# SSD's weighted inputs as broadcast products on GpSimd, and four loads of the merge on ScalarE's queue

## The chip, the cores and the metric

The kernel runs on one core of a Trainium2 chip. Its time is device microseconds of one execution; of several runs the median is given. The engines are TensorE (PE), VectorE (DVE), ScalarE (ACT), GpSimd (POOL) and SyncE (SP). Each takes its instructions in order from a queue of its own, and waits for the others by semaphores. SyncE only issues DMAs here; ScalarE and GpSimd issue some among their own work.

## The reference, cut to what matters

One step of a hybrid layer on 576 frames (512 of a prompt and 64 of a sample), width 1024, float32:

```python
h = x + 0.5 * swiglu(rmsnorm(x, norm_ffn1), w_ffn1_in, w_ffn1_out)
h = h + mixer(rmsnorm(h, norm_mix))
h = h + 0.5 * swiglu(rmsnorm(h, norm_ffn2), w_ffn2_in, w_ffn2_out)
# mixer(u):
parts = split_cols(u @ w_in, IN_SIZES)          # one projection for three branches and three gates
merged = (sigmoid(g_ssd) * (y_ssd @ w_proj_ssd) + sigmoid(g_att) * (y_att @ w_proj_attn)
          + sigmoid(g_ml) * (y_ml @ w_proj_mlstm))
return merged @ w_out
# one chunk of the SSD scan (16 heads of 64 in 4 groups, state 128), per group and head:
y = (cb * lmat * dtc) @ xc + exp(cum) * (cc @ h)
wd = exp(last - cum) * dtc
h = exp(last) * h + einsum('bsh,bsn,bshp->bhpn', wd, bc, xc)
```

The change concerns the last two lines, where each input row is weighted by `wd` before it is multiplied into the state, and the start of the sum `merged`.

## The kernel before

The program runs through a first feed-forward (to some 600 us), the mixer's input projection with the three branches (to 1210), the merge with its output projection, and a second feed-forward. Frames lie along the free axis as 512 + 64 columns, or in two halves of 288.

Every large product is made of three: the weight and the activation are each split into a rounded part and a rest (`split`, L288 a cast on ScalarE and L289 a subtraction on VectorE; `ph`, `pl` for weights, `TH`, `TL` for activations), and `acc` collects TH x ph, TL x ph and TH x pl in L616. The projection saves multiplications by working on two tiles at a time with seven sums of weight blocks (as Strassen does). The sums come from an accumulating DMA (L461) and from additions on GpSimd (L472, `wy`); SyncE loads the raw blocks (L467, L237 into `wr`) some operands ahead, into rings of 5 (`wr`), 4 (`wx`), 2 (`wy`) and 6 (`ph`, `pl`). When a product's bank is complete, it is emptied by ScalarE (`uv`, L533, or `g`, L540) or by VectorE (L542); TensorE takes the bank again a few products later.

The branches are generators. While the projection for later tiles runs, a job of attention (a), mLSTM (m) or SSD (s) advances by one `yield` after each product (`tick`, L575), in the order a0 a1 m0 s0 a2 a3 s1 m1 s2 m2 s3 m3. This is the order in which the code is written; a scheduler then reorders each engine's instructions by modelled times, so that an edit in one place can change the order of all engines.

`ssd(g)` does one group of the SSD in two halves j of two heads (8 halves in all). Line numbers are those of the kernel before: the weights `wd` come from rows that a DMA brings from DRAM (`R<-scr_rows`, L181, L1175) by L1209 and L1210 on VectorE and an Exp on ScalarE; x is transposed (L1218, L1222) and multiplied by dt into `xd` (L1219, L1223); L1228 makes the weighted copy `xw` on ScalarE; L1234 to L1237 and L1242 make decay factors on ScalarE, L1238 and L1239 multiply them on GpSimd. The state matmul L1252 reads `xw`, L1255 and L1260 update the state, L1274 to L1287 make the output. Other work that stands near: L1049 masks of mLSTM (VectorE, from `R`), L1152 the convolution's last step (ScalarE).

`merge()` multiplies the branches' outputs, stored in DRAM as `ys`, by the three projections. Its first four loads (`heads(0, 1, 2, 3)`, L1340) bring attention's outputs, 288 KB each; they are split into YH and YL (L288, L289) for the products L260. GpSimd loads the gates beside it (`g<-gs`, L1354).

Of the kernel before, what the change touches and what calls it, by code (L numbers as in the profile page):

```python
# [27 lines left out]
AF = mybir.ActivationFunctionType  # L28
ALU = mybir.AluOpType
# [5 lines left out]
CH = [(0, 128), (128, 128), (256, 128), (384, 128), (512, 64)]  # L35
# [46 lines left out]
class Hybrid:  # L82
# [1085 lines left out]
    def ssd(self, g, t):  # L1168
        nc = self.nc
# [12 lines left out]
        h4 = lambda ap: ap.rearrange("p c (h e) -> p c h e", e=64)  # L1182
# [4 lines left out]
        for c in range(4):  # L1187
# [3 lines left out]
                                op=ALU.mult)  # L1191
# [7 lines left out]
        for j in range(2):  # L1199
# [4 lines left out]
            wd = self.unit([128, 5, 2], "wd", 2)  # L1204
            el = self.unit([128, 5, 2], "el", 2)
            nc.gpsimd.memset(wd[:, 4, :], 0.0)
            for r in range(2):
# [3 lines left out]
                                        op=ALU.subtract)  # L1211
# [3 lines left out]
            xd, xw = self.t("t", (128, 5, 128)), self.t("t", (128, 5, 128))  # L1215
            ps = self.ps("x")
            for c in range(4):
# [4 lines left out]
            nc.tensor.transpose(ps[:64, :128], x[:, 515:579], self.ident)  # L1222
            nc.vector.tensor_tensor(h4(xd[:64, 4:5, :]), ps[:64, :128].rearrange("p (c h e) -> p c h e", h=2, e=64),  # L1223
                                    self.TM[:64, 4:5, d0:d0 + 2].unsqueeze(3).broadcast_to([64, 1, 2, 64]), op=ALU.mult)
            for c, (a, n) in enumerate(CH):
                for r in range(2):
                    hs = slice(r * 64, (r + 1) * 64)
                    nc.scalar.activation(xw[:n, c, hs], xd[:n, c, hs], AF.Copy, scale=wd[:n, c, r:r + 1])  # L1228

            for r in range(2):  # L1230
                e = cum[r]
# [14 lines left out]
            for c, (a, n) in enumerate(CH):  # L1246
# [9 lines left out]
                else:  # L1256
                    h = states[c]
                    for r in range(2):
                        hs = slice(r * 64, (r + 1) * 64)
# [68 lines left out]
    def merge(self):  # L1328
        nc, tc = self.nc, self.tc
        def rows():  # L1330
            return [Rows(self.mp.tile([128, T], F32R, name=f"Y{v}", tag=f"{v}{i}", bufs=1) for i in range(8)) for v in "HL"]

        ys = [self.mp.tile([128, T], F32, name="y", tag="y", bufs=4) for _ in range(4)]
        YH, YL = rows()
        merged = self.mp.tile([128, 8, T], F32, name="merged")
        ZH, ZL = [Rows(self.xp.tile([128, T], F32R, name=f"Z{v}{i}") for i in range(8)) for v in "HL"]

        def load(src, eng=nc.gpsimd):
            y = ys.pop() if ys else self.mp.tile([128, T], F32, name="y", tag="y", bufs=4)
            eng.dma_start(y, src)  # L1340
            return y


        gates = deque((8 * b + n) for b in (1, 2, 0) for n in range(8))
        loaded = deque()

        def fill(n):
            while gates and len(loaded) < n:
                i = gates.popleft()
                if i in STAY:  # L1350
                    y = self.stay[i]
                else:
                    y = self.t("g")
                    self.last = nc.gpsimd.dma_start(y, self.gs[i]).ins  # L1354
                loaded.append((i, y))

        def put(n, branch):

            box = {}

            def go(h, ps, sl):
                if not box:
                    i, box["t"] = loaded.popleft()
                    assert i == 8 * branch + n
                    fill(5)
                t = box["t"][:, sl]
                o = merged[:, n, sl] if branch == 1 else t
                nc.vector.scalar_tensor_tensor(o, t, 1.0, ps, op0=ALU.add, op1=ALU.mult)
                if branch != 1:
                    nc.gpsimd.tensor_tensor(merged[:, n, sl], merged[:, n, sl], t, op=ALU.add)  # L1370
            return go

        def heads(*which, eng=nc.gpsimd):
            for i in which:
                y = load(self.ys[i], eng)
                if i < 4:
                    self.split(y, YH[:, i, :], YL[:, i, :])
                else:
                    self.scaled(y, C_ML - 4, YH, YL, i, slice(0, T), tile=True)

        def half(branch, which):
            w = ("w_proj_attn", "w_proj_mlstm")[branch - 1]
            for m in which:
                self.gemm([((w, 0, 512, m * 256, 256), [(e * 128, put(2 * m + e, branch)) for e in range(2)])],
                          YH, YL, k0=4 * branch - 4)

        def ssd(which):

            for k in which:
                y = load(self.ys[8 + k])  # L1390
                nc.vector.scalar_tensor_tensor(y, y, self.cst[:, C_GS + k:C_GS + k + 1], self.rs,
                                               op0=ALU.mult, op1=ALU.mult)
                self.split(y, ZH[:, k, :], ZL[:, k, :])

        with tc.high_priority(offset=1500):
            heads(0, 1, 2, 3, eng=nc.sync)
        fill(5)
        half(1, (0, 1))
        heads(4, 5, 6)
        half(1, (2, 3))  # L1400
        heads(7)
        ssd(range(2))
        half(2, (0, 1))
        ssd(range(2, 5))
        half(2, (2, 3))
        ssd(range(5, 8))
        tiles = [(("w_proj_ssd", 0, 1024, n * 128, 128), [(0, put(n, 0))]) for n in range(8)]
        self.gemm(tiles[:4], ZH, ZL)

        with tc.issue_after(self.last):  # L1410
            for k in range(0, 8, 2):
                nc.gpsimd.dma_start(self.R1[:, k:k + 2, :], self.xs[:, k:k + 2, :])
        self.gemm(tiles[4:5], ZH, ZL)
        self.gemm(tiles[5:], ZH, ZL, half_major=True)
        XH, XL = rows()
        for a, n in HALVES:
            for k in range(8):
                sl = slice(a, a + n)
                self.split(merged[:, k, sl], XH[:, k, sl], XL[:, k, sl])

        def res(n):
            def go(h, ps, sl):

                nc.vector.scalar_tensor_tensor(self.R1[:, n, sl], ps, 0.5, self.R1[:, n, sl], op0=ALU.mult, op1=ALU.add)
            return go
        tiles = [(("w_out", 0, 1024, n * 128, 128), [(0, res(n))]) for n in range(8)]
        self.gemm(tiles[:3], XH, XL, half_major=True)
        self.gemm(tiles[3:5], XH, XL)
        self.gemm(tiles[5:], XH, XL, half_major=True)
# [179 lines left out]
```

## Time and profile before

| what | value |
|---|---|
| median of 3 runs | 1942.54 us (1939.22 to 1944.31) |
| profiled execution: time, span | 1944.79 us, 1943.1 us |
| TensorE busy, mean granted clock | 1887.2 us (97%), 0.991 |
| VectorE, ScalarE, GpSimd busy | 1524.6 us (78%), 1089.5 us (56%), 680.1 us (35%) |
| mean DMA rate | 152 GB/s |

The profile is of one execution. A row of a timeline gives the start, the time that the group of like instructions took, what it was, how often, and in brackets how long the engine stood idle just before and what released it. A row `PE acc <- ACT uv` among the waits says that TensorE stood until ScalarE's `uv` copy had emptied a bank. The granted clock is a share of full speed. What stands idle or slow on TensorE adds to the time nearly one for one here, since it is busy for 97% of the span.

### The profile page before, as it was taken

The page shows a single profiled execution, that of the slowest core. Times are in us where ns is not written, and L with a number is a line of the kernel's source. Part 1 is how long each engine was busy: PE and PEld are TensorE (multiplying, and loading weights), DVE is VectorE, ACT ScalarE, POOL GpSimd, SP SyncE. Part 2 cuts the span into 40 slices and gives each one's busy share as a digit, 9 for nine tenths or more (in the row PEclk, how much of TensorE's full clock was granted, in tenths as well). Part 3 has the DMA queues.
Part 4 walks back from the last instruction along what each step waited for, and adds up shares of the span by engine and source line. Part 5 has one row for each costly group of instructions (what it writes and reads, how often), then busy time and mean ns, then how long its engine had stood idle before and what let it go on. Part 6 is the DMA issues. An engine that isn't in the chain of part 4 may idle for free. (4 is left out here: it accounts for less than half of the span.)

```text
span 1943.1 us, 37678 instructions
## 1 busy us (share of the span) xinstructions
PE 1887.2 (97%) x13901; PEld 1823.6 (94%) x13901; DVE 1524.6 (78%) x2715; ACT 1089.5 (56%) x2486; POOL 680.1 (35%) x656
## 2 busy tenths in 40 slices
PE   9999999999999999999999998999999999999998
PEld 8899999999999878888888888999999999999998
DVE  8998998988768767667777775745898888988865
ACT  4554654655544777767675765324555455554544
POOL 5343333333202234323435353440233334334311
PEclk9999999999999999899999999999999999999999
DMA  7267666666742545753667557742236666666631
GB/s 241 74 160 173 159 163 163 159 172 163 185 131 80 156 117 159 200 147 108 183 165 183 155 152 213 241 143 88 77 99 165 163 157 172 166 157 167 159 94 60
DMA packets 129440, 294.69 MB, mean 152 GB/s; under 512 B 14289, under 2 KB 26193, under 8 KB 129257
## 3 DMA queue, kind: packets, MB, share of 16 engines
q1 hardware_dynamic: 100072, 205.67, 32.7%
q0 software_dynamic: 19696, 72.10, 20.5%
q10 hardware_dynamic: 9488, 14.53, 2.6%
q8 instruction: 109, 1.79, 0.4%
q14 instruction: 75, 0.61, 0.1%
HBM read 272.87 MB, written 19.38 MB: 150 GB/s over the span
## 5 line engine op out<-in xcount | busy, mean ns | idle before, releaser
L616 PE MATMUL acc<-TH,ph 128*128 128x288 f32 x3220 | 968.0, 301 | 27.4 <-ACT uv L533 11.8
L616 PE MATMUL acc<-TL,ph 128*128 128x288 f32 x3220 | 955.4, 297 | 0.6 <-DVE TL L289 0.6
L616 PE MATMUL acc<-TH,pl 128*128 128x288 f32 x3220 | 955.0, 298 | 1.0 <-DVE pl L289 0.9
L616 PEld LDWEIGHTS acc<-TH,ph 128*128 128x128 f32 x3220 | 607.5, 189 | 46.9 <-ACT uv L533 15.5
L616 PEld LDWEIGHTS acc<-TL,ph 128*128 128x128 f32 x3220 | 609.4, 189 | 4.9 <-issue 3.7
L616 PEld LDWEIGHTS acc<-TH,pl 128*128 128x128 f32 x3220 | 608.4, 189 | 4.8 <-DVE pl L289 2.2
L289 DVE TENSOR_TENSOR pl<-wr,ph 128x512 fp32r<-128x512 f32 x471 | 429.4, 919 | 76.9 <-ACT ph L288 64.5
L288 ACT CAST ph<-wr 128x512 fp32r<-128x512 f32 x471 | 287.9, 620 | 267.9 <-PE acc L616 141.3
L289 DVE TENSOR_TENSOR pl<-wx,ph 128x512 fp32r<-128x512 f32 x390 | 328.1, 845 | 44.5 <-ACT ph L288 37.9
L288 ACT CAST ph<-wx 128x512 fp32r<-128x512 f32 x390 | 237.4, 621 | 201.3 <-POOL wx L472 110.2
L472 POOL TENSOR_TENSOR wx<-wx,wr 128x512 f32<-128x512 f32 x160 | 246.3, 1539 | 188.2 <-DVE pl L289 150.4
L461 POOL DMA_DIRECT2D wx<-in_sblk x115 | 101.6, 901 | 524.1 <-DMA wx<-in_sblk 154.7
L260 PE MATMUL acc<-YH,ph 128*128 128x256 f32 (+1 forms) x768 | 226.5, 298 | 6.3 <-ACT YH L288 5.8
L260 PE MATMUL acc<-YL,ph 128*128 128x320 f32 (+1 forms) x768 | 227.1, 297 | 2.3 <-DVE YL L339 1.9
L260 PE MATMUL acc<-YH,pl 128*128 128x256 f32 (+1 forms) x768 | 226.5, 296 | 0.1
L260 PEld LDWEIGHTS acc<-YH,ph 128*128 128x128 f32 x768 | 145.4, 190 | 6.9 <-ACT YH L288 5.9
L260 PEld LDWEIGHTS acc<-YL,ph 128*128 128x128 f32 x768 | 145.4, 189 | 3.5 <-DVE YL L339 3.3
L260 PEld LDWEIGHTS acc<-YH,pl 128*128 128x128 f32 x768 | 145.2, 189 | 0.3 <-DVE pl L289 0.3
L472 POOL TENSOR_TENSOR wy<-wx,wr 128x512 f32<-128x512 f32 x35 | 56.2, 1605 | 136.0 <-DVE pl L289 120.0
L655 DVE SCALAR_TENSOR_TENSOR R<-acc,R 128x288 f32<-128x288 f32 x168 | 75.7, 450 | 18.6 <-PE acc L616 18.1
L288 ACT CAST TH<-g 128x288 fp32r<-128x288 f32 x120 | 51.6, 434 | 59.8 <-POOL g L641 34.6
L289 DVE TENSOR_TENSOR pl<-wy,ph 128x512 fp32r<-128x512 f32 x70 | 59.8, 857 | 29.6 <-ACT ph L288 26.6
(320 smaller groups left out, 2393.4 us busy)
## 6 DMA issues: line engine op xcount, KB each, us to landing
wr<-in_sblk SPq DMA_DIRECT2D x345, 256.0 KB, 3.6
wx<-in_sblk SPq DMA_DIRECT2D x115, 512.0 KB, 3.8
wx<-in_sblk POOLq DMA_DIRECT2D x115, 512.0 KB, 6.8
wr<-in_wblk SPq DMA_DIRECT2D x126, 256.0 KB, 3.0
R<-scr_rows ACTq DMA_DIRECT2D x12, 576.0 KB, 5.9
gs<-g SPq DMA_DIRECT2D x20, 288.0 KB, 4.5
g<-gs POOLq DMA_DIRECT2D x20, 288.0 KB, 3.9
y<-ys POOLq DMA_DIRECT2D x12, 288.0 KB, 3.8
```

Source lines behind the costliest of these rows:

```text
L260: nc.tensor.matmul(ps[:, :n], wt[:, wsl], xx[:, k0 + k, a:a + n], start=(k == 0 and i == 0), stop=(k == nk - 1 and i == 2))
L288: self.nc.scalar.copy(hi, src)
L289: self.nc.vector.tensor_tensor(lo, src, hi.bitcast(F32), op=ALU.subtract)
L461: return {"x12": x12, "src": src}, lambda: nc.gpsimd.dma_start(x12, src[:, 1:3, :], accum_op=ALU.add)
L472: add = lambda o, one, two: self.nc.gpsimd.tensor_tensor(o, one, two, op=ALU.add)
L616: self.nc.tensor.matmul(ps, wt[:, wsl], xx[:, kk, :], start=(start and kk == 0 and i == 0), stop=(kk == 3 and i == 2), skip_group_check=True)
L655: self.nc.vector.scalar_tensor_tensor(o, ps, scale, o, op0=ALU.mult, op1=ALU.add)
```

## The change

In `ssd` the ten ScalarE instructions of a half, one per chunk and head, become two GpSimd products, in which `wd` is broadcast along the 64 columns of a head; the small chunk's product reads 64 partitions. In `merge` the first four loads are issued from ScalarE's queue instead of SyncE's. The changed kernel is one line shorter, so lines behind 1228 have numbers that are lower by 1 there.

```diff
-            for c, (a, n) in enumerate(CH):
-                for r in range(2):
-                    hs = slice(r * 64, (r + 1) * 64)
-                    nc.scalar.activation(xw[:n, c, hs], xd[:n, c, hs], AF.Copy, scale=wd[:n, c, r:r + 1])
+            for n, cs in ((128, slice(0, 4)), (64, slice(4, 5))):
+                nc.gpsimd.tensor_tensor(h4(xw[:n, cs, :]), h4(xd[:n, cs, :]),
+                                        wd[:n, cs, :].unsqueeze(3).broadcast_to([n, cs.stop - cs.start, 2, 64]), op=ALU.mult)
...
         with tc.high_priority(offset=1500):
-            heads(0, 1, 2, 3, eng=nc.sync)
+            heads(0, 1, 2, 3, eng=nc.scalar)
```

The scheduler orders all engines differently from SSD's group 0 (766 us of the trace before) to the end of the mixer. In the feed-forwards the order stays. Three places follow.

ScalarE and VectorE in SSD group 0. ScalarE before, at about 767 to 776 us (`ph` casts are for weights, `uv` and L540 empty banks):

```order
L288 CAST ph<-wy 128x512
L540 ACTIVATE g<-acc 128x288
L1228 ACTIVATE t<-t,wd 128x64 x8
L1228 ACTIVATE t<-t,wd 64x64 x2
L288 CAST ph<-wy 128x512
L533 ACTIVATE uv<-acc 128x288 x2
L288 CAST ph<-wx 128x512
L533 ACTIVATE uv<-acc 128x288
L1255 COPY st<-ps_s 128x128
L288 CAST ph<-wr 128x512
L288 CAST ph<-wx 128x512
```

ScalarE there in the changed kernel:

```order
L288 CAST ph<-wy 128x512
L540 ACTIVATE g<-acc 128x288
L288 CAST ph<-wy 128x512
L533 ACTIVATE uv<-acc 128x288 x2
L288 CAST ph<-wx 128x512
L533 ACTIVATE uv<-acc 128x288
L288 CAST ph<-wr 128x512
L288 CAST ph<-wx 128x512
L288 CAST ph<-wr 128x512
L1254 COPY st<-ps_s 128x128
L288 CAST ph<-wr 128x512
```

The burst of L1228 is gone from between the casts and the copies out of the banks, and the state copy (L1255, now L1254) stands later. VectorE before, at about 783 to 792 us, in the group's second half:

```order
L289 TENSOR_TENSOR pl<-wy,ph 128x512 x2
L1260 SCALAR_TENSOR_TENSOR st<-st,el,ps_s 128x64 x2
L1209 TENSOR_TENSOR wd<-R_60,TM 128x4
L1275 SCALAR_TENSOR_TENSOR g<-g,cst,ps_v 128x512
L1210 TENSOR_TENSOR wd<-R_60,TM 64x1
L1209 TENSOR_TENSOR wd<-R_60,TM 128x4
L1210 TENSOR_TENSOR wd<-R_60,TM 64x1
L542 SCALAR_TENSOR_TENSOR g<-acc,uv 128x288
L1260 SCALAR_TENSOR_TENSOR st<-st,el,ps_s 128x64 x2
```

VectorE there in the changed kernel:

```order
L289 TENSOR_TENSOR pl<-wy,ph 128x512
L1275 SCALAR_TENSOR_TENSOR g<-g,cst,ps_s 128x64
L1281 TENSOR_TENSOR R_60<-ps_x,R_60 128x448
L1259 SCALAR_TENSOR_TENSOR st<-st,el,ps_s 128x64 x2
L542 SCALAR_TENSOR_TENSOR g<-acc,uv 128x288
L1209 TENSOR_TENSOR wd<-R_60,TM 128x4
L1210 TENSOR_TENSOR wd<-R_60,TM 64x1
L1209 TENSOR_TENSOR wd<-R_60,TM 128x4
L1210 TENSOR_TENSOR wd<-R_60,TM 64x1
L1274 SCALAR_TENSOR_TENSOR g<-g,cst,ps_v 128x512
```

L542 stood behind the four instructions that make `wd` from the DMA's rows, and now stands ahead of them. In group 2 L542 stood right behind L1049's five before, and now several rows ahead of them, with another one some rows behind.

GpSimd in SSD group 1, before (L1238 and L1239 are the burst of decay products, L472 weight sums):

```order
L1238 TENSOR_TENSOR R_60<-R_60,t 128x512 x4
L1239 TENSOR_TENSOR R_60<-R_60,t 64x64 x4
L472 TENSOR_TENSOR wy<-wy,wr 128x512
L461 DMA wx<-in_sblk 128x1024
L1206 MEMSET wd 128x2
L472 TENSOR_TENSOR wy<-wx,wr 128x512
L472 TENSOR_TENSOR wy<-wy,wr 128x512
```

GpSimd there in the changed kernel:

```order
L1237 TENSOR_TENSOR R_60<-R_60,t 128x512 x4
L1238 TENSOR_TENSOR R_60<-R_60,t 64x64 x4
L472 TENSOR_TENSOR wy<-wy,wr 128x512
L461 DMA wx<-in_sblk 128x1024
L1226 TENSOR_TENSOR t<-t,wd 128x512
L1226 TENSOR_TENSOR t<-t,wd 64x128
L472 TENSOR_TENSOR wy<-wx,wr 128x512
L1206 MEMSET wd 128x2
L472 TENSOR_TENSOR wy<-wy,wr 128x512
```

The two products of L1226 stand behind the burst, a weight sum and a DMA issue. On TensorE the first state matmul of this half stood 32 product matmuls behind the transposes of x before; now 56 product matmuls and 8 of L1273 stand between.

SyncE and ScalarE at the start of the merge. SyncE before (`y` are the loads):

```order
L1124 DMA ys_76<-g 128x576
L237 DMA wr<-in_wblk 128x512 x4
L1340 DMA y<-ys_69 128x576
L1340 DMA y<-ys_70 128x576
L1340 DMA y<-ys_71 128x576
L1340 DMA y<-ys_72 128x576
L237 DMA wr<-in_wblk 128x512 x54
```

ScalarE there in the changed kernel:

```order
L288 CAST ph<-wr 128x512
L544 ACTIVATE g<-g 128x288
L288 CAST ph<-wr 128x512
L1339 DMA y<-ys_69 128x576
L1339 DMA y<-ys_70 128x576
L1339 DMA y<-ys_71 128x576
L1339 DMA y<-ys_72 128x576
L540 ACTIVATE g<-acc 128x288
L1304 COPY rs<-ps_x 128x256
L1304 COPY rs<-ps_x 128x320
L288 CAST YH<-y 128x576 x4
```

The loads have left SyncE, whose weight loads L237 now follow one another without a break, and stand on ScalarE behind a weight cast (`ph`, a ring of six) and ahead of the last bank's copy (L540) and the casts of `y`.

## Rows read from the trace of the kernel before

**Rows 1.** The page's busy shares, and two of its groups (busy, mean ns, idle before).

```profile
PE 1887.2 (97%) x13901; PEld 1823.6 (94%) x13901; DVE 1524.6 (78%) x2715; ACT 1089.5 (56%) x2486; POOL 680.1 (35%) x656
...
L289 DVE TENSOR_TENSOR pl<-wx,ph 128x512 fp32r<-128x512 f32 x390 | 328.1, 845 | 44.5 <-ACT ph L288 37.9
...
L472 POOL TENSOR_TENSOR wy<-wx,wr 128x512 f32<-128x512 f32 x35 | 56.2, 1605 | 136.0 <-DVE pl L289 120.0
```

**Rows 2.** TensorE's waits over 766 to 1215 us: us in total, times, longest us.

```profile
PE acc L616 <- ACT uv L533: 10.9, 10, 2.9
PE acc L616 <- DVE g L542: 3.3, 3, 1.6
```

**Rows 3.** The instructions of line 1228: duration ns min/median/max, first and last start us, forms.

```profile
L1228 ACT ACTIVATE t<-t,wd x80: 333/338/352, 767.8 to 1154.8; 128x64 f32<-128x64 f32 x64, 64x64 f32<-64x64 f32 x16
```

**Rows 4.** ScalarE's timeline: start us, us, line, operation, count, [idle before <-releaser].

```profile
767.81 2.51 ACT L1228 ACTIVATE t<-t,wd 128x64 f32<-128x64 f32 x10 [3.14 <-DVE t L1219]
...
940.22 0.58 ACT L1228 ACTIVATE t<-t,wd 64x64 f32<-64x64 f32 x2
...
944.67 0.69 ACT L1242 ACTIVATE R<-R 128x576 f32<-128x576 f32 x1 [2.03 <-DMA R<-scr_rows]
...
1209.17 0.62 ACT L288 CAST ph<-wr 128x512 fp32r<-128x512 f32 x1 [1.54 <-issue]
```

**Rows 5.** TensorE's timeline, in the same columns.

```profile
771.18 0.40 PE L616 MATMUL acc<-TH,ph 128*128 128x288 f32 x1 [0.78 <-ACT uv L533]
...
791.96 0.40 PE L616 MATMUL acc<-TH,ph 128*128 128x288 f32 x1 [1.59 <-DVE g L542]
...
920.81 0.38 PE L1252 MATMUL ps_s<-t 128*128 128x128 f32 x2
...
942.54 0.40 PE L616 MATMUL acc<-TH,ph 128*128 128x288 f32 x1 [1.06 <-ACT g L540]
...
946.23 0.40 PE L616 MATMUL acc<-TH,ph 128*128 128x288 f32 x1 [0.95 <-ACT uv L533]
...
1045.66 0.40 PE L616 MATMUL acc<-TH,ph 128*128 128x288 f32 x1 [1.49 <-DVE g L542]
...
1099.39 0.40 PE L616 MATMUL acc<-TH,ph 128*128 128x288 f32 x1 [2.87 <-ACT uv L533]
...
1216.49 0.85 PE L260 MATMUL acc<-YH,ph 128*128 128x256 f32 x2 [5.78 <-ACT YH L288]
```

**Rows 6.** VectorE's timeline.

```profile
790.17 0.49 DVE L1209 TENSOR_TENSOR wd<-R,TM 128x4 f32<-128x4 f32 x1 [3.96 <-DMA R<-scr_rows]
...
1039.27 2.58 DVE L289 TENSOR_TENSOR pl<-wx,ph 128x512 fp32r<-128x512 f32 x1
...
1044.21 1.03 DVE L1049 TENSOR_SCALAR P<-R,TM 128x128 f32<-128x128 f32 x5 [2.36 <-DMA R<-scr_rows]
```

**Rows 7.** Windows behind two waits: busy us by engine, granted clock, DMA share, GB/s.

```profile
792.00:804.00 12.00, 12.00 (x53) 10.81 (x54) 9.30 (x22) 7.59 (x22) 4.56 (x5) 0.57 0.73 200
1100.00:1104.00 4.00, 4.00 (x21) 4.00 (x20) 3.63 (x6) 2.07 (x7) 1.74 (x1) 0.58 0.06 17
```

**Rows 8.** GpSimd's products of lines 1238, 1239 and 1054: ns min/median/max, first and last start.

```profile
L1238 POOL TENSOR_TENSOR R<-R,t x16: 1283/1750/1769, 761.9 to 1131.0; 128x512 f32<-128x512 f32 x16
...
L1239 POOL TENSOR_TENSOR R<-R,t x16: 312/318/776, 768.3 to 1133.6; 64x64 f32<-64x64 f32 x16
...
L1054 POOL TENSOR_TENSOR P<-P,mask x4: 1284/1292/2621, 721.1 to 1153.7; 128x512 f32<-128x512 f32 x4
```

**Rows 9.** GpSimd's timeline in SSD group 1.

```profile
923.79 0.87 POOL L461 DMA_DIRECT2D wx<-in_sblk  x1
```

**Rows 10.** SyncE's issues at the start of the merge.

```profile
1207.57 2.08 SPq L1340 DMA_DIRECT2D y<-ys  x4
```

**Rows 11.** DMA issues over 1200 to 1220 us: count, KB each, median us to landing.

```profile
y<-ys SPq DMA_DIRECT2D x4, 288.0 KB, 8.9
y<-ys POOLq DMA_DIRECT2D x3, 288.0 KB, 3.8
```

## The prediction

> **What bounds the kernel now.** I read the busy shares of the page first: TensorE is busy for 1887.2 of 1943.1 us, 97%, and all else sits beside it [rows 1]. So the change can give only what TensorE stands idle, or runs at a low clock, in the stretch that it touches: from 766 us, where the first edited instruction runs, to 1220, where the merge has started. The waits of TensorE over 766 to 1215 us come next. Nearly all are one thing: a product waits for its accumulator bank, which ScalarE (`uv`, 10.9 us in 10 waits) or VectorE (L542, 3.3 us in 3) has not emptied yet [rows 2]. It hardly ever waits for weights: GpSimd's weight sums stood idle for 136.0 us until a buffer came free [rows 1], so the operand side has slack. The question is what stood ahead of the late evacuations on their in-order queues; the timelines of ScalarE and VectorE show it, and the windows show what TensorE's clock did afterwards.
>
> **Part 1: 80 scalings leave ScalarE.** They are 80 of about 338 ns [rows 3]; as they overlap by their starts, the ten of one half take 2.51 us [rows 4], and the 8 halves 20.1 us of ScalarE. ScalarE is not the bound, so this is worth only the evacuations behind it:
> - At 771.18 TensorE waits 0.78 us for `uv`; ten scalings of 2.51 us stood just ahead [rows 4, 5]. In the new order they are gone: 0.78.
> - At 942.54 it waits 1.06 us for L540; the 0.58 us pair stood a few places ahead [rows 4, 5]. A second place at 1156 is like it: 2 x 0.58 = 1.2.
>
> The scheduler has also dealt the rest of the mixer anew, and this is worth more:
> - At 791.96 TensorE waits 1.59 us for L542, because VectorE stood 3.96 us at L1209 for a DMA, ahead of it [rows 5, 6]. In the new order L542 stands ahead of L1209. Behind this wait the granted clock was 0.57 on average over 792 to 804 us [rows 7], mostly at its lower level (1.2 of 2.4 GHz): against the full one this lost 12 x 0.43 = 5.2 us. Together 6.8.
> - At 1045.66 it waits 1.49 us, with VectorE 2.36 us at L1049 for a DMA [rows 5, 6]; L542 is now some rows ahead of L1049 there: 1.5.
> - At 946.23 it waits 0.95 us for `uv`, because ScalarE stood 2.03 us at L1242 for a DMA [rows 4, 5]; one more, of 0.80, is like it. The `uv` copies now stand elsewhere: 1.75.
> - At 1099.39 it waits 2.87 us for `uv` behind decay and convolution work, and the clock was 0.58 over 1100 to 1104 [rows 5, 7]. With `uv` ahead of L1152 I count half the wait, 1.45, and 4 x 0.42 = 1.7 of clock: 3.1.
>
> Sum: 0.8 + 1.2 + 6.8 + 1.5 + 1.75 + 3.1 = 15.1 us that can go. These are gaps that the scheduler's own times did not foresee (late DMAs above all), and the new order is made with the same times, so new ones will arise at other places. What comes back lies between 0 and 15.1; no row says which, and I take half, 7.6.
>
> **Part 2: 16 products come to GpSimd.** The trace has no such product. Its nearest rows are L1238, 128x512 of two tiles in SBUF, at 1.28 to 1.77 us, and L1054, 128x512 with a broadcast operand, at 1.28 to 2.62; for the small one 0.31 to 0.78 by L1239 [rows 8]. I take 1.6 + 0.6 = 2.2 per half, 17.6 us in all (bounds 12.7 and 27). GpSimd is 35% busy, and its slack hides this, except where TensorE comes for the product: the state matmul, which now waits for GpSimd. In group 1 GpSimd's burst ends with the DMA issue at 923.79 + 0.87 [rows 9]; with 1.6 the product is there at 926.3. TensorE came to this matmul at 920.81 [rows 5]; now 24 product matmuls and 8 of L1273 more stand ahead, at 1887.2/13901 = 0.136 us each, so it comes at 925.2 and waits 1.1. The same reckoning leaves 0.8 to 1.6 us to spare in the other groups; I add as much for one of them: 2.2. Bounds: 0, and the first rival.
>
> Two GpSimd products also run against VectorE. At 1039.27 one weight subtraction took 2.58 us beside GpSimd's products, where the mean of its kind is 0.85 [rows 1, 6]: some 1.7 us late, hidden by the slack of the operands.
> The Trainium skill, "SBUF — State Buffer", section "Who interferes with whom", says that a VectorE instruction with two SBUF inputs and a GpSimd instruction that reads SBUF exclude each other for a whole instruction. The 2.58 us agrees with it. It is the third rival below.
>
> **Part 3: the four loads on ScalarE's queue.** Before, SyncE issued them from 1207.57 on, 2.08 us for the four, and TensorE stood 5.78 us, to 1216.49, for the cast of the first; a load took 8.9 us to land [rows 5, 10, 11]. In the new order they stand behind a weight cast, that waits for a buffer which the stream's last product frees; that cast ran at 1209.17 before [rows 4]. So the issue starts about 1209.7, 2.1 us later. Against this they no longer queue behind SyncE's weight loads. If the queue was the delay, 1209.7 plus the 3.8 us that such loads take on GpSimd's queue [rows 11] gives 1213.5, some 2 us earlier than before (1207.57 + 8.9 = 1216.5 for the median one, the first sooner). If it was the engines that all queues share, they land 2.1 us later. Ends -2.1 and +2.1; as three queues then share engines on which before two did, the first load in a short queue profits: I take -1.
> The Trainium skill, "DMA: Bandwidth & Descriptors", section "Issuing engines are not separate DMA queues", says that transfers of all issuing engines run on the same 16 engines, and that another issuer saves only issue time. By it this part would be near +2. No run so far shows which.
>
> **Sum.** -15.1 + 7.6 + 2.2 - 1 = -6.3 us. The profiled execution took 1944.8, so 1938.5 for one like it; the median of the three runs is 1942.5, 2.3 lower, which gives 1936.2, and that is the forecast.
>
> **The rivals.**
> - *GpSimd late, slower.* If the 1.75 us of L1238's slow half is the rule and each burst slips 2 us more, the four first halves wait about 3.1, 1.2, 0.8 and 0.4 us, 5.5 in all, and two of these cost the clock 1.7 to 5.2 us each [rows 7]: 9 to 16. It decides from the point where the product is 2 us behind its matmul in more than one group. With the re-dealt gaps all back it gives 1942.5 + 10 = 1952. For it: the short margins, and L1054's 2.62 us [rows 8]. Against it: GpSimd's idle time, and that the second halves have one burst less ahead. 15%.
> - *All gaps come back.* -15.1 + 15.1 + 2.2 - 1: 1943.7, no change. For it: ScalarE had idle time already, and 13 of the 15.1 us hang on the new deal rather than on the removed work. Against it: 2 us hang on the removed work alone. 17%.
> - *VectorE kept out.* If each of the 8 large products holds back one subtraction by 1.7 us [rows 6] and an L542 stands right behind in a third of them, 8 x 1.7 / 3 = 4.5 us comes on top: 1941, no change. For it the one row; against it that before 16 products of L1238 and many more ran beside VectorE at little cost to TensorE. 6%.
> - *Nothing comes back.* -15.1 + 1.1 - 1 = -15.0, 1927.5. For it: TensorE has waited at these places for DMAs that now have no evacuation behind them. 22%.
>
> **How the numbers follow.** The forecast has the remaining 40%, with 1931 to 1942 as its own range. About 0.3% is what a measurement of this kernel can tell from no change, here 5.8 us: faster is below 1936.7, slower above 1948.4. Faster: all of "nothing comes back" and somewhat over half of the forecast, 0.22 + 0.23 = 0.45. Slower: the first rival and some of the second, 0.15 + 0.03 = 0.18. The rest, 0.37, is no change. The range reaches from 1925 (nothing back, and the merge at its -2.1 and more) to 1949, and leaves the worst of the first rival out.
>
> **What would show it.** ScalarE's busy time falls by about 20 us, GpSimd's rises by about 18; the new line's large form has a mean of 1.3 to 1.8 us. The waits for `uv` and L542 over 766 to 1215 us fall from 14.2 to about 10 us, and the windows behind 792 and 1100 are back at full clock. A row of the state matmul waiting for GpSimd appears, with about 2 us. The wait for the first cast of the merge falls from 5.8 to about 4.8. I am wrong if waits of that kind stay at 14 us or above, if that row has 5 us or more, or if a 0.50 clock stands behind two new gaps.

## The result: 0.23% slower, and the profile after

The changed kernel takes 1944.74 us (median of 20 runs, 1940.87 to 1948.59), the kernel before 1940.20 us in 20 runs (1935.13 to 1945.46): ratio 1.0023, 95% interval 1.0014 to 1.0032, or some 4.5 us more. The two profiled executions stand the other way round: the one after has 1941.88 us, near the bottom of its runs, and the one before, on which the prediction's sum rests, 1944.79, near the top of its own. So the spans of the two profiles must not be set against each other; what can be compared is where TensorE stands still, and where in the program time goes. TensorE's timelines, before and then after, show its first transposition of x, up to which its order is the same:

```profile
763.63 0.60 PE L1218 MATMUL ps_x<-ident,g 128*128 128x128 f32 x4
761.45 0.60 PE L1218 MATMUL ps_x<-ident,g 128*128 128x128 f32 x4
```

The merge's first product starts at 1216.49 [rows 5] and 1212.73, and from there to the end the two take 726.6 and 727.5 us. What the change can have moved lies between: 452.9 us before and 451.3 after. So this pair of profiles does not show the loss; the runs do.

The work moved as planned. The page after, busy us by engine, answers to [rows 1]: ScalarE has 21.6 us less, GpSimd 16.5 more, and VectorE, whose instructions are the same 2715, 14.5 more.

```profile
PE 1881.3 (97%) x13901; PEld 1822.2 (94%) x13901; DVE 1539.1 (79%) x2715; ACT 1067.9 (55%) x2406; POOL 696.6 (36%) x672
```

The new products' own line after (duration ns min/median/max, starts, forms, then who waited): nothing stands behind the last line, so no engine ever waited for them.

```profile
L1226 POOL TENSOR_TENSOR t<-t,wd x16: 393/1114/1487, 770.0 to 1145.3; 128x512 f32<-128x512 f32 x8, 64x128 f32<-64x128 f32 x8
...
who waited for it (us, times):
```

TensorE's waits after over 766 to 1215 us (total, times, longest) answer to [rows 2]. The waits for `uv` are as long as before in fewer pieces, those for L542 hardly shorter. Two kinds that were short before have grown: L1113 (0.6 before) and the sums of L306 (0.7 before). The cast of YH is in this list because the merge starts earlier; before, its wait of 5.78 us ended behind this window [rows 5].

```profile
PE acc L616 <- ACT uv L533: 10.8, 8, 3.0
PE acc L260 <- ACT YH L288: 4.3, 1, 4.3
PE ps_x L1119 <- DVE Q L1113: 3.4, 1, 3.4
PE acc L616 <- DVE g L542: 3.0, 4, 1.6
PE ps_x L330 <- POOL sm L306: 2.9, 2, 1.9
PE acc L616 <- ACT g L540: 2.0, 1, 2.0
```

TensorE's timeline after, its longest waits in brackets, against [rows 5]. The waits of 771, 792, 946 and 1099 us are gone. In their place are others, and most are longer.

```profile
935.38 0.40 PE L616 MATMUL acc<-TH,ph 128*128 128x288 f32 x1 [1.97 <-ACT g L540]
...
1040.48 0.60 PE L616 MATMUL acc<-TH,ph 128*128 128x288 f32 x1 [2.64 <-ACT uv L533]
...
1066.11 0.37 PE L616 MATMUL acc<-TH,ph 128*128 128x288 f32 x1 [1.64 <-DVE g L542]
...
1089.55 0.80 PE L1119 MATMUL ps_x<-ident,Q 128*128 128x128 f32 x2 [3.40 <-DVE Q L1113]
...
1152.27 0.40 PE L616 MATMUL acc<-TH,ph 128*128 128x288 f32 x1 [2.99 <-ACT uv L533]
...
1212.73 1.54 PE L260 MATMUL acc<-YH,ph 128*128 128x256 f32 x5 [4.25 <-ACT YH L288]
```

Behind the three longest of these ahead of the merge the granted clock was low (windows after: start and end, length, busy us by engine, clock, DMA share, GB/s), as it was behind two waits before [rows 7]. Within these windows it was 0.50 over 1041 to 1043.5, 1089 to 1095 and 1153.5 to 1156.5.

```profile
1040.00:1048.00 8.00, 7.52 (x46) 7.52 (x47) 7.13 (x14) 5.56 (x15) 4.49 (x4) 0.79 0.09 32
1088.00:1096.00 8.00, 6.45 (x28) 5.70 (x29) 4.19 (x9) 5.93 (x16) 3.61 (x3) 0.57 0.27 93
1152.00:1160.00 8.00, 7.73 (x47) 7.74 (x48) 7.22 (x15) 4.24 (x11) 2.96 (x3) 0.79 0.21 46
```

What made the wait at 1040.48 is on ScalarE's timeline after: L1067 of the mLSTM, with its table load, stands one cast behind the issue of the rows' load (L181), waits 3.17 us for it, and the `uv` copy waits behind L1067.

```profile
1030.95 0.39 ACTq L181 DMA_DIRECT2D R<-scr_rows  x1
1033.11 0.62 ACT L288 CAST ph<-wr 128x512 fp32r<-128x512 f32 x1 [2.55 <-PE acc L616]
1033.74 1.28 ACT L1067 ACT_TABLE_LOAD   x1
1038.20 0.29 ACT L1067 ACTIVATE wc<-TM,R 128x1 f32<-128x1 f32 x1 [3.17 <-DMA R<-scr_rows]
...
1040.03 0.69 ACT L533 ACTIVATE uv<-acc 128x288 f32<-128x288 f32 x2
```

Before, eight scalings stood between the issue (at 1036.31) and the reader, and 2.03 us of the load's flight were spent on them (ScalarE's timeline before):

```profile
1039.39 2.03 ACT L1228 ACTIVATE t<-t,wd 128x64 f32<-128x64 f32 x8 [0.60 <-DVE t L1219]
1041.42 1.28 ACT L1067 ACT_TABLE_LOAD   x1
1044.21 1.03 ACT L1067 ACTIVATE wc<-TM,R 128x1 f32<-128x1 f32 x5 [1.50 <-DMA R<-scr_rows]
```

The waits at 935 and 1152 us have L1067 ahead of them in the same way. The longest, at 1089.55, came by way of VectorE: it waited 1.85 us for rows at L1209, to 1084.88, and behind that came L305, GpSimd's L306 (2.29 us) and, at 1089.08, L1113. So my first theory after the result (A) was: the scalings had covered the flight of these loads, and with them gone, readers of the rows stand ahead of copies out of the banks. The rivals: B, the merge's loads cost the time; C, any new order of the same instructions moves the time by some us; D, GpSimd's products hold VectorE up; and, added later, E, without the scalings the scheduler puts readers of the rows nearer to loads that land late.

### The profile page after: what moved, and what is told of

Its sections match the earlier page's. It is cut to its first block, busy times and chain, and to the rows that moved or that the text cites. A ratio compares the mean times of both kernels' runs of the same rounds, so it can differ in the third digit from the quotient of the medians.

```text
span 1940.2 us, 37592 instructions
## 1 busy us (share of the span) xinstructions
PE 1881.3 (97%) x13901; PEld 1822.2 (94%) x13901; DVE 1539.1 (79%) x2715; ACT 1067.9 (55%) x2406; POOL 696.6 (36%) x672
## 5 line engine op out<-in xcount | busy, mean ns | idle before, releaser
L616 PE MATMUL acc<-TH,ph 128*128 128x288 f32 x3220 | 967.2, 301 | 27.2 <-ACT uv L533 11.7
L616 PE MATMUL acc<-TL,ph 128*128 128x288 f32 x3220 | 956.6, 297 | 0.6 <-DVE TL L289 0.6
L616 PE MATMUL acc<-TH,pl 128*128 128x288 f32 x3220 | 954.8, 297 | 0.6 <-DVE pl L289 0.6
L616 PEld LDWEIGHTS acc<-TH,ph 128*128 128x128 f32 x3220 | 606.9, 189 | 45.1 <-ACT uv L533 14.1
L616 PEld LDWEIGHTS acc<-TL,ph 128*128 128x128 f32 x3220 | 608.9, 189 | 5.4 <-issue 4.4
L616 PEld LDWEIGHTS acc<-TH,pl 128*128 128x128 f32 x3220 | 608.3, 189 | 5.7 <-issue 3.8
L289 DVE TENSOR_TENSOR pl<-wr,ph 128x512 fp32r<-128x512 f32 x471 | 444.8, 952 | 72.9 <-ACT ph L288 59.0
L289 DVE TENSOR_TENSOR pl<-wx,ph 128x512 fp32r<-128x512 f32 x390 | 316.6, 816 | 35.0 <-ACT ph L288 28.6
L472 POOL TENSOR_TENSOR wx<-wx,wr 128x512 f32<-128x512 f32 x160 | 246.0, 1538 | 187.2 <-DVE pl L289 149.1
L472 POOL TENSOR_TENSOR wy<-wx,wr 128x512 f32<-128x512 f32 x35 | 55.0, 1573 | 130.4 <-DVE pl L289 110.7
L655 DVE SCALAR_TENSOR_TENSOR R<-acc,R 128x288 f32<-128x288 f32 x168 | 75.7, 451 | 19.2 <-PE acc L616 18.9
L641 POOL TENSOR_TENSOR g<-g,P 128x288 f32<-128x288 f32 x56 | 62.9, 1124 | 39.4 <-ACT P L640 39.4
```

The costliest lines, as they stand in the source:

```text
L289: self.nc.vector.tensor_tensor(lo, src, hi.bitcast(F32), op=ALU.subtract)
L472: add = lambda o, one, two: self.nc.gpsimd.tensor_tensor(o, one, two, op=ALU.add)
L616: self.nc.tensor.matmul(ps, wt[:, wsl], xx[:, kk, :], start=(start and kk == 0 and i == 0), stop=(kk == 3 and i == 2), skip_group_check=True)
L641: nc.gpsimd.tensor_tensor(s["g"][:, 1, :], s["g"][:, 1, :], a, op=ALU.mult)
L655: self.nc.vector.scalar_tensor_tensor(o, ps, scale, o, op0=ALU.mult, op1=ALU.add)
```

## The experiments

Each ratio is against the kernel before, run beside it, with its 95% interval. The clock is TensorE's mean granted clock over all executions of the kernel; before has 0.992 in each set of runs that lists it. The last three columns are from each profile: TensorE's idle time between 752 and 1204 us, summed over the brackets of its timeline, how many of these waits have 1.5 us or more, and its idle time from the first transposition of x (L1218) to the merge's first product, the wait for that included. (x2's merge starts before 1204; its wait of 5.8 us there is left out of the first of the three. In n1 and x1 a wait for the sums ahead of the merge, 1.9 and 2.7 us, is still within it.)

| kernel | scalings on ScalarE | products on | ratio | clock | idle us, 752 to 1204 | long | idle to the merge, us |
|---|---|---|---|---|---|---|---|
| before | yes | none | 1 | 0.992 | 19.2 | 2 | 25.8 |
| after | no | GpSimd | 1.0023 [1.0014, 1.0032] | 0.989 | 23.0 | 6 | 30.2 |
| e1 products only | no | GpSimd | 1.0016 [1.0004, 1.0028] | 0.989 | 24.3 | 5 | 32.0 |
| e2 loads only | yes | none | 0.9999 [0.9985, 1.0013] | 0.992 | 20.9 | 1 | 24.6 |
| n1 same work, chunks last to first | yes | none | 0.9989 [0.9976, 1.0001] | 0.992 | 21.9 | 3 | 25.2 |
| n3 same work, head by head | yes | none | 0.9978 [0.9967, 0.9988] | 0.993 | 19.2 | 1 | 26.4 |
| c1 copies as cover | no | GpSimd | 1.0015 [1.0003, 1.0027] | 0.989 | 22.5 | 4 | 29.3 |
| f7 mLSTM's exps tied later | no | GpSimd | 1.0035 [1.0022, 1.0047] | 0.988 | 24.7 | 6 | 32.6 |
| b7 the same tie in before | yes | none | 1.0034 [1.0020, 1.0047] | 0.991 | 24.6 | 4 | 31.9 |
| z1 no weighting | no | none | 1.0025 [1.0014, 1.0035] | 0.990 | 20.6 | 4 | 28.8 |
| p2 products beside scalings | yes | GpSimd, unread | 1.0007 [0.9994, 1.0021] | 0.992 | 18.5 | 1 | 25.7 |
| d1 products on VectorE | no | VectorE | 1.0041 [1.0025, 1.0058] | 0.990 | 22.9 | 4 | 30.3 |
| m1 small products first | no | GpSimd | 1.0031 [1.0017, 1.0044] | 0.990 | 23.5 | 4 | 30.2 |
| p1 products, dead scalings | yes, unread | GpSimd | 1.0051 [1.0038, 1.0064] | 0.989 | 22.8 | 5 | 30.7 |
| x0 no row loads | yes | none | 1.0005 [0.9995, 1.0015] | 0.991 | 20.7 | 3 | 27.9 |
| x2 no row loads, head by head | yes | none | 0.9947 [0.9931, 0.9962] | 0.992 | 16.4 | 0 | 22.1 |
| x1 no row loads | no | GpSimd | 0.9973 [0.9963, 0.9983] | 0.991 | 20.4 | 4 | 23.1 |
| x3 no row loads, small first | no | GpSimd | 0.9964 [0.9950, 0.9977] | 0.991 | 18.4 | 3 | 24.9 |

From the merge's first product to the end every one of these profiles takes 725.7 to 728.2 us, so what tells the kernels apart arises ahead of it. Of those that load the rows, the five that are not slower (before, e2, n1, n3, p2) idle 24.6 to 26.4 us to the merge, with a clock of 0.992 or 0.993; the nine slower ones idle 28.8 to 32.6 us, with 0.988 to 0.991. A clock lower by 0.003 costs at most some 1940 x 0.003 = 5.8 us by estimate, less where it falls on idle time. Idle time does not turn into time one for one either: e1 idles 7.4 us more to the merge than e2 and takes 3.6 us more for it (452.7 against 449.1 us).

### Which half of the change: e1 and e2

e1 is the changed kernel with `eng=nc.sync` in the merge; e2 is the kernel before with

```diff
-            heads(0, 1, 2, 3, eng=nc.sync)
+            heads(0, 1, 2, 3, eng=nc.scalar)
```

> Only the products on GpSimd; the loads stay on SyncE, and up to the merge every engine's order is that of the changed kernel. Theory A (the new order holds copies out of the banks behind waits for the rows' DMA): the whole loss is here, +3 to +6 us against before, and TensorE shows the waits of 2 to 3.4 us that the changed kernel has at some 935, 1040, 1089 and 1152 us. Theory B (the loads on ScalarE's queue cost it): within 1 us of before.

> Only the four loads on ScalarE's queue; the scalings stay on ScalarE and the order differs from before only at the merge. Theory A: within 1 us of before; the wait for the first cast stays at 4 to 6 us. Theory B: +3 to +5 us, with a wait there of 8 us or more.

The loads cost nothing that can be told, and B falls; the products alone are slower, with waits at the same products of TensorE. e2 shows two things more. It has the order of before up to the merge, so it is a second execution of the wait at 791.96 [rows 5]. VectorE waited there for the rows again, but TensorE's wait (timeline of e2) was 0.43 us, and the clock behind it (window of e2) full:

```profile
795.21 0.40 PE L616 MATMUL acc<-TH,ph 128*128 128x288 f32 x1 [0.43 <-DVE g L542]
```

```profile
796.00:808.00 12.00, 11.60 (x79) 10.04 (x78) 9.40 (x22) 8.79 (x26) 4.56 (x5) 1.00 0.81 216
```

And at the merge ScalarE of e2 issues the four loads from 1210.98 us on, where SyncE before did from 1207.57 on [rows 10] and the projection's last product (L616) started 1.8 us earlier; but they land after a median of 6.0 us instead of 8.9 [rows 11], and TensorE's wait is 4.92 us instead of 5.78 (timelines of ScalarE and TensorE, and the DMA issues over 1200 to 1225 us, in e2):

```profile
1210.98 1.78 ACTq L1340 DMA_DIRECT2D y<-ys  x4
```

```profile
1217.23 1.81 PE L260 MATMUL acc<-YH,ph 128*128 128x256 f32 x6 [4.92 <-ACT YH L288]
```

```profile
y<-ys ACTq DMA_DIRECT2D x4, 288.0 KB, 6.0
```

The other pair, the changed kernel against e1, has a wait of 4.25 us instead of 5.32, but there the loads land after a median of 10.2 us on either queue. So the wait is shorter in both pairs, and why it is remains open.

### The same work in other orders: n1 and n3

n1 takes the chunks of L1225 last to first; n3 swaps the two loops:

```diff
-            for c, (a, n) in enumerate(CH):
-                for r in range(2):
+            for r in range(2):
+                for c, (a, n) in enumerate(CH):
```

> Before with the five chunks of each weighted input taken last to first: the same 80 instructions on ScalarE, the same work everywhere, but some 600 rows of ScalarE's order change. Theory C (any new order of the same work moves the time by some us, up or down): 2 us or more away from before. If only what an engine has to do counts: within 1 us.

> Before with the 80 scalings taken head by head instead of chunk by chunk: the same work once more in another order. Theory C: a third value, more than 1.5 us from before or from the order with the chunks last to first. If only the work counts: within 1 us of before.

n3 does exactly what before does and is 0.22% faster, clear of its interval, and faster than both kernels of this case. n1 lies between, its interval just touching 1. C holds here: a mere swap of loops moves the time by as much as the change does.

### Cover put back, and the reader moved: c1, f7 and b7

c1 adds, to e1, eight copies of 128x64 per mLSTM head behind the issue of the rows' load. f7 changes e1 (and b7 changes before) so:

```diff
-                nc.scalar.activation(o, ps, AF.Copy, scale=scale)
+                self.uv = nc.scalar.activation(o, ps, AF.Copy, scale=scale)
...
-        nc.scalar.activation(D[:, :512], D[:, :512], AF.Exp)
+        with self.tc.issue_after(self.uv.ins):
+            nc.scalar.activation(D[:, :512], D[:, :512], AF.Exp)
...
-        for c, (a, n) in enumerate(CH):
+        with self.tc.issue_after(self.uv.ins):
+            for c, (a, n) in enumerate(CH):
...
```

> Products on GpSimd, loads on SyncE, and eight copies of 128x64 on ScalarE per mLSTM head that nobody reads, placed behind the issue of the rows' load: 32 more instructions of ScalarE. Theory A: where they, or copies out of the banks, now stand between the issue and the first reader, the wait for the rows is covered again, so the time is 2 to 5 us below that of the products alone although ScalarE does more. Against it (ScalarE's work is what counts): 0 to 3 us above the products alone.

> Products on GpSimd, loads on SyncE, and the mLSTM's first instructions on ScalarE that read the rows (L1051, L1052, L1067, with their table load) tied behind the last copy out of a bank that the code has issued by then, so that they no longer stand ahead of it. Theory A (such waits ahead of the copies cost the time): TensorE's waits at some 935, 1040 and 1152 us (2.0 + 2.6 + 3.0 us in the products alone) go, and the time is 3 to 7 us below the products alone, that is from 3.5 us below before to 0.5 above it. Theory D (GpSimd's products hold VectorE up, whatever the order): it stays at +2 to +5 us. Theory C (any new order is a draw): anywhere within 4 us of before.

> The same tie in the kernel before, whose 80 scalings stay on ScalarE. There these instructions waited only 1.7 us for the rows, since eight scalings of 2.03 us stood between the issue and them. Theory A: 0 to 2 us below before. Theory C: within 4 us of before, to either side.

c1 cannot be told from e1, where A had it 2 to 5 us below. f7 is the clear miss. Its three target waits did go (their sizes in the expectation are those of the changed kernel; e1 has 1.5, 3.0 and 2.3), and yet it is slower: 6.8 us above before, beyond C's 4 us too. So is b7, 6.6 us above before, which also misses both. TensorE's timeline in f7 shows what came: waits for VectorE's results in the branches, and for the sums at the end, where L306 on GpSimd came late.

```profile
937.98 0.46 PE L1253 MATMUL ps_s<-t 128*128 128x128 f32 x2 [3.24 <-DVE st L1261]
...
966.82 0.83 PE L1089 MATMUL ps_v<-t,P 128*128 128x129 f32 x4 [1.85 <-DVE P L1061]
...
994.82 1.28 PE L1121 MATMUL ps_x<-ident,Q 128*128 128x128 f32 x4 [1.68 <-DVE Q L1115]
...
1075.05 0.40 PE L616 MATMUL acc<-TH,ph 128*128 128x288 f32 x1 [2.22 <-ACT uv L533]
...
1215.34 1.01 PE L330 MATMUL ps_x<-ident,sm 128*128 128x128 f32 x3 [6.38 <-POOL sm L306]
```

The last is GpSimd's doing (its timeline in f7):

```profile
1213.96 0.58 POOL L1355 DMA_DIRECT2D g<-gs  x1 [6.30 <-DMA ys<-g]
1214.56 0.73 POOL L306 TENSOR_TENSOR sm<-sm,mhalf 128x2 f32<-128x2 f32 x1
```

VectorE's waits over 752 to 1205 us in f7 are 27.6 us for the rows' loads (16.7 + 10.9), against 13.7 before and 19.5 in e1, while ScalarE's fell from 16.4 in e1 to 10.8: the wait was moved to another engine, not removed. VectorE's waits in f7, e1 and before, two rows each:

```profile
DVE wd L1211 <- DMA R<-scr_rows: 16.7, 4, 5.8
DVE P L1049 <- DMA R<-scr_rows: 10.9, 3, 6.9
...
DVE P L1049 <- DMA R<-scr_rows: 12.1, 3, 5.7
DVE wd L1209 <- DMA R<-scr_rows: 7.4, 5, 2.2
...
DVE wd L1209 <- DMA R<-scr_rows: 7.4, 4, 4.0
DVE P L1049 <- DMA R<-scr_rows: 6.3, 3, 2.9
```

In b7 VectorE's waits rose in the same way, from 13.7 to 20.5 us. So A named where the waits stood, but not what sets their sum: in this narrow form it falls. VectorE's waits for the rows go with the loss over the other kernels too: 18.0 to 27.6 us in the nine slower ones, 7.3 to 14.1 in before, e2, n3 and p2. But n1 has 20.6 and is not slower, and each number is from one profile, so this is a sign and no proof.

### GpSimd's load, ScalarE's load: z1, p2, d1, m1 and p1

z1 leaves the ten scalings out and lets L1252 read `xd`. p2 is before with the changed kernel's two products added, into a tile `xq` that nobody reads; p1 is the reverse, the products read and the scalings written to `xq`. d1 has `nc.vector` for `nc.gpsimd` in the products, m1 the order `((64, slice(4, 5)), (128, slice(0, 4)))`; p1, d1 and m1 keep the loads on SyncE.

> Before without the weighting: the 80 scalings are left out, and the state matmul reads the unweighted inputs, so states and outputs of the SSD are other numbers. No product comes to GpSimd. Theory D (GpSimd's 16 products hold VectorE up): 0 to 5 us below before, with VectorE's busy time in the mixer (752 to 1205 us) at 317 to 322 us as before. Theory E (the scalings' absence from ScalarE makes the order worse, as waits lose their cover): 3 to 5 us above before, like the products alone. Theory C (a draw): within 4 us of before.

> Before with its 80 scalings, which TensorE reads, and the 16 products on GpSimd as well, into a buffer that nobody reads. Theory D: 2 to 5 us above before, VectorE's busy time over 752 to 1205 us at 325 to 330 us instead of 317 to 322. Theory E: within 1.5 us of before. Theory C: within 4 us of before.

> The 16 products on VectorE instead of GpSimd, the loads on SyncE. VectorE gets 8 x (0.7 + 0.2) = 7 us of work of its own, and nothing more runs on GpSimd. Theory D: 2 to 5 us below the products on GpSimd, that is within 2 us of before. Theory E: 3 to 5 us above before. Theory C: within 4 us of before.

> The products on GpSimd with the small one of each half ahead of the large one: the work of the products alone in another order (some 500 rows of ScalarE's order differ). Theory D: again 2 to 5 us above before. Theory E: the same. Theory C: anywhere within 4 us of before.

> The products on GpSimd, which TensorE reads, loads of the merge on SyncE, and the 80 scalings kept on ScalarE into a buffer that nobody reads: 20 us more of ScalarE than the products alone. Theory E: within 1.5 us of before, 2 to 4 us below the products alone, though it does more. If ScalarE's work costs what it takes or nothing: as the products alone or above, +3 to +6 us.

D falls, by z1 and d1 above all: it had them no slower than before and within 2 us of it, and they are 4.9 and 8.0 us above. p2 has the products' whole load and cannot be told from before (its interval reaches some 4 us above it), although its VectorE is the busiest of all kernels that load the rows (third column of busy times, p2 over 752 to 1204 us):

```profile
752.00:1204.00 452.00, 432.31 (x3185) 396.09 (x3183) 332.24 (x637) 312.22 (x843) 202.46 (x201) 1.00 0.62 166
```

z1 has less to do on every engine concerned, no product anywhere, and is 0.25% slower than before (the same window of z1):

```profile
752.00:1204.00 452.00, 430.90 (x3150) 397.24 (x3149) 310.45 (x630) 291.26 (x759) 177.64 (x174) 0.98 0.60 161
```

The kernel before has 316.25 us of VectorE in that window, the changed one 327.41:

```profile
752.00:1204.00 452.00, 432.30 (x3151) 397.31 (x3152) 316.25 (x631) 310.41 (x838) 181.62 (x177) 0.98 0.61 163
752.00:1204.00 452.00, 427.61 (x3160) 396.29 (x3159) 327.41 (x635) 291.34 (x757) 198.21 (x197) 0.98 0.60 163
```

z1, m1 and d1 have the sign that E expected, though m1 (6.0 us above before) and d1 are beyond its sizes, and all three are beyond C's 4 us. So C's draw is wider than it said, and here it mostly lost. p1 contradicts the form in which work on ScalarE as such keeps the order good: with 80 dead scalings it is the slowest of all, 9.9 us above before, outside both of its ranges. p1 and p2 give every engine the same numbers of instructions; they differ in which copy L1252 reads, and in the order. No row of either trace shows the state matmul waiting for its copy, and yet p1 is 0.44% slower than p2. So what an engine has to do does not settle the time.

### The rows' loads taken away: x0 to x3

x0 (from before) and x1 (from e1) replace L181 and L1175 so; x2 and x3 do the same to n3 and m1:

```diff
-        self.nc.scalar.dma_start(self.R1[:, i:i + 2, :], self.rows(r0, 128, step))
+        self.nc.gpsimd.memset(self.R1[:, i:i + 2, :], -3000.0)
...
-                nc.scalar.dma_start(rows[j][2][r * 64:(r + 1) * 64, :], self.rows(4 * g + 2 * j + r, 64))
+                nc.gpsimd.memset(rows[j][2][r * 64:(r + 1) * 64, :], -3000.0)
```

> Before with all loads of the rows replaced by a constant that GpSimd writes (so the mixer's branches compute other numbers); no engine can wait for those loads any more. Theory E (readers of the rows stand too near to the issue of loads that land late): faster than before by 3 to 10 us. If the rows' loads play no part: within 2 us of before.

> The products on GpSimd, loads of the merge on SyncE, and the rows' loads replaced by the same constant. Theory E: the penalty of taking the scalings off ScalarE is gone, within 1.5 us of the same kernel with scalings, or below it. If the penalty has another cause: 3 to 6 us above that kernel, as with the loads.

> The scalings on ScalarE, head by head instead of chunk by chunk, and the rows' loads replaced by the constant: the work of the kernel without row loads in another order. Theory E (the rows' loads turn the products' gain into a loss): within 2 us of its first order, so -1 to +3 us against before. Theory C (a draw): anywhere within 5 us of before.

> The products on GpSimd with the small one first, and the rows' loads replaced by the constant. Theory E: 2 us or more below the kernel with scalings and no row loads (in the same call), that is -7 to -2 us against before. Theory C: no nearer to that than to before, anywhere within 5 us of before.

x0 misses: without any wait for rows before is not faster. (The constant is new work for GpSimd, 196.4 instead of 181.6 us over 752 to 1204, so these kernels differ from theirs by more than the waits.) x1 is 0.27% faster than before, which by itself would have spoken for E. The second orders undo that: x2, with scalings, is the fastest kernel of all, some 10 us below before where E and C had allowed at most 1 and 5, and the two orders of one work, x0 and x2, lie 0.58% (11 us) apart. x3, some 7 us below before, is above x2 where E had it 2 us or more below, and beyond C's 5 us. What is left for E is that both kernels with products gained from the loads' removal (1.0016 and 1.0031 became 0.9973 and 0.9964), 0.43% and 0.67%; of those with scalings one gained 0.31% (n3 to x2) and the other nothing (before to x0).

## Why the prediction was wrong, point by point

- *What bounds the kernel.* Right: TensorE stays at 97%, and the slower kernels differ by more idle time ahead of the merge and a lower mean clock. Most of the idle time is waits for banks. That idle time adds to the time nearly one for one, as the part on the profile before says, these traces do not bear out (e1 against e2).
- *The scalings' own price* (20.1 us of ScalarE, worth 2.0 us to TensorE). ScalarE's busy time fell by 21.6 us. The wait at 771.18 did go; in the stretch of 942 one of 1.97 us stands instead.
- *The clock behind 791.96, 5.2 us of 15.1.* Mis-sized. Three quarters of the largest term (5.2 of 6.8) came from one execution: with the same order e2 had 0.43 us and full clock there. A stretch of low clock that one profile shows once is not a price per run. At the product of 1099.39, where 3.1 us were counted, e2 waited 1.43 us instead of 2.87, with the clock full behind it. The same profile was also 4.6 us above the median of the 20 runs of before; the median of the three runs then known put it at 2.3.
- *"What comes back lies between 0 and 15.1; I take half."* This is the step that failed. Most of the named waits went, but more came back than had gone: TensorE's idle time to the merge rose from 25.8 us (24.6 in e2) to 30.2 (32.0 in e1), and the waits of 1.5 us or more between 752 and 1204 from 2 (1 in e2) to 6 (5), behind three of which (two in e1) the clock was low. The mean clock of the runs fell from 0.992 to 0.989. With nothing for GpSimd and -0.9 for the merge, the measured +4.5 asks for some 20 us back instead of 7.6, or some 15 if the 5.2 us of clock were never there to gain (estimates from the prediction's own sum): more than had gone, either way. The upper bound had no ground. The removed waits were no reserve that a new order draws on; a new order makes its own, and before and n3, x0 and x2 show that even the same work gives orders 0.2 to 0.6% apart.
- *The signs that were named.* The waits for `uv` and L542 fell from 14.2 to 13.8 us instead of about 10, just short of the limit of 14. The clock at 0.50 stood behind three new gaps, one more than was to count as wrong.
- *GpSimd's products.* 1.6 + 0.6 us were forecast for a half; no product took more than 1.49, and GpSimd rose by 16.5 us for 17.6. The 2.2 us of waiting for them did not arise at all, and the rival "GpSimd late" was wrong.
- *VectorE kept out.* VectorE was busy for 11 us more in the mixer, where 8 x 1.7 = 13.6 was the reckoning, and one subtraction beside the product at 914.05 took 3.08 us. This agrees with the exclusion that the Trainium skill, "SBUF — State Buffer", section "Who interferes with whom", describes. But the 11 us are no fixed price (p1, with the same products, has 317.43 us over 752 to 1204), and a cost in time is not shown: p2 bears 16 us more and cannot be told from before.
- *The merge* (-1 of a range from -2.1 to +2.1). Right in place and size for the wait: -0.9 us in e2 and -1.1 in the changed kernel against e1; the other end, +2.1, did not come. The reason given, a shorter queue, is open: the loads landed sooner in e2 (6.0 us instead of 8.9), but not in the changed kernel (10.2 us, as in e1). In the time nothing of it can be told (0.9999). In the changed kernel 2.2 us more than before went to the sums ahead of the first cast (2.9 against 0.7 us for `sm` of L306); that comes with the products, since e1 has 2.4.
- *The rival "all gaps come back"* (1943.7, 17%) came nearest to the measured 1944.7, in part by luck: it is +1.2 us on a base of 1942.5, where +4.5 on 1940.2 was measured, and the 2.2 us for GpSimd in it did not arise. It should have been the forecast, with a spread to both sides: nothing in the order said which waits a new deal would bring, and only 2 of the 15.1 us hung on the work that was removed.

What stays open is why this change lost rather than won. All seven kernels in which ScalarE has no scalings and the rows are loaded (after, e1, c1, f7, z1, d1, m1) are slower than before, by 0.15 to 0.41%, while n1, n3, e2 and p2 are not. The late rows' loads seem to take part in it, by VectorE's waits for them and by the gains of x1 and x3, but that is argued, not shown. p1 and b7 keep the scalings and are slower too, and with up to 0.6% between two orders of one work I can't tell a rule of the scheduler from a run of bad draws.

## What to carry to other kernels

Where a scheduler orders all engines anew, an edit off the critical path can buy a draw among orders, as here; size that draw first, with two or three versions that do the same work in another order, before a gain of the same size is put down to the edit. A wait that an edit removes counts fully only if the order around it stays; if not, expect as many waits as before at other places. Set the mean granted clock of all runs beside the ratios: among the kernels that load the rows it told the slower ones from the others here, where the clock of a single profile had misled. And look at what the removed work had covered: at 1039 us, eight of the scalings had stood between the issue of a load and its first reader.

## What was not expected of the hardware

Two executions with the same order up to the merge (before and e2) differ by a whole low-clock stretch: 0.57 over 792 to 804 us in one, 1.00 over 796 to 808 in the other, behind waits of 1.59 and 0.43 us for the same copy. The changed kernel and e1 have one order of TensorE up to the merge, and their waits stand at the same products; but behind the wait of 2.64 us at 1040.48 the clock was 0.79 in the one, and behind the still longer wait at the same product it was full in the other (timeline and window of e1):

```profile
1043.20 0.40 PE L616 MATMUL acc<-TH,ph 128*128 128x288 f32 x1 [3.00 <-ACT uv L533]
```

```profile
1043.00:1051.00 8.00, 7.62 (x55) 7.14 (x55) 7.33 (x14) 5.37 (x15) 4.51 (x4) 1.00 0.14 38
```

And VectorE's busy time in the mixer grew by 11 us though not one of its instructions was added, and p2 shows 332.24 us against 316.25 without a loss of time that can be told (1.0007, at most 1.0021).
